# Heads two at a time on the two halves of the array, and a new order of loads, modulation and down products in a two-block transformer kernel

## The chip, the cores and the metric

The kernel runs on one core of one Trainium2 chip, in one launch. A time is the device time of a run in microseconds. The kernel before takes 1041.57 us, the median of three runs (1040.76 to 1041.62). The core's engines are TensorE (PE, with the loading of its weights listed apart as PEld), VectorE (DVE), ScalarE (ACT), GpSimd (POOL) and SyncE (SP), which issues nearly all of the transfers.

## The reference, cut to what matters

One sequence of 256 tokens, width 1024, passes through two transformer blocks. The first has two SwiGLU feed-forwards and, between them, a mixer of causal attention and a convolution; each of the three is modulated by numbers that are computed from a vector `c`. The second has a mixer with two attention branches and gates, a feed-forward with squared ReLU, and a gated projection at the end.

```
# block 1
mod = (silu(c) @ w_ada + b_ada).reshape(3, 3, 1024)
x = x + 0.5 * mod[0, 2] * swiglu(modulate(x, ...), w13[0], w2[0])    # 1024 -> 2 x 2816 -> 1024
x = x + mod[1, 2] * hybrid_mixer(modulate(x, ...), ...)              # 8 heads, values 64 wide
x = x + 0.5 * mod[2, 2] * swiglu(modulate(x, ...), w13[1], w2[1])
# block 2
z = rmsnorm(x, norm_mix_g) @ w_in            # qa ka va | qb kb vb | ga gb
y_a = mixer_a(qa, ka, va, ...) @ w_out_a     # 8 heads of 128
y_b = mixer_b(qb, kb, vb, rel_bias) @ w_out_b
# mixer_b: 4 heads of 64 in each of 3 dilated windows, softmax with a bias
#          by distance; the three are joined by their log-sum-exp
x = x + (sigmoid(ga + b) * y_a + sigmoid(gb + b) * y_b) @ w_out
x = x + square(relu(rmsnorm(x, norm_mlp_g) @ w_ff1)) @ w_ff2         # 1024 -> 4096 -> 1024
x = x + sigmoid(rmsnorm(x, norm_ple_g) @ w_ple_gate) * (p @ w_ple)
return rmsnorm(x, final_norm_g)
```

## The kernel before, in words

The activations lie transposed, 128 features on the partitions and 256 tokens in the row, in eight slices `d` of 128 features. Each fp32 weight that is used in a large product is split into two parts: ScalarE casts it to a high part `hi` (line 141), VectorE subtracts for a low part `lo` (line 142). A product is then three matmuls with 128x128 weights and 256 columns (`mm3`, lines 152 to 154). The small matmuls of the attention heads are plain fp32.

The stages on the time axis: start (to 31 us), first feed-forward (31 to 226), first mixer (226 to 399), second feed-forward (399 to 594), second mixer (594 to 827, with branch B in 704 to 764), the feed-forward of block 2, here the mlp (827 to 1002.6), and the end with the gate `pg` and the last norm.

The order of the instructions on each engine is set by the framework's scheduler from the order in which the code is written and from modelled times. Tiles come from pools with a fixed number of buffers; a transfer or a computation that needs a new buffer waits till an old one is free.

*Feed-forwards* (`stream_ffn`, lines 382 to 412). In each iteration `make` computes two slices of the hidden layer: products `gu` (or `u`), then `s` on ScalarE, `m` on VectorE, and the split of `m` into `mh` (ScalarE, line 174) and `ml` (VectorE, line 175). `second` multiplies the slices of the iteration before into the eight slices of the output, two to each of four banks `acc0` to `acc3`. Its weight, the down weight, is loaded right behind `make` (line 407). After the last `second`, `finish` adds each slice to the residual (line 416 or 421), from which the sum of squares for the next norm is built: `squares` (line 331) on ScalarE, the adding of six of them on POOL (line 333), and two that go to PE's `nrm_ps` directly (line 342). Where the next norm's factor comes later (`gained`), `hh` and `hl` (lines 377, 378) follow from the residual at once.

*Modulation.* `ada_rest` spreads parts of `silu(c) @ w_ada` over the iterations: 2 MB of weights from SyncE's queue, eight multiplications by VectorE (lines 267, 269), two casts to bf16 pieces `ada_b` on ScalarE (line 273) with two subtractions on VectorE (line 274), and, an iteration later, twelve matmuls `ada_ps` with one column (line 279). Its tuple says how many parts begin at each iteration.

*Heads.* `_stages` runs scores, transposition and values of successive heads as a pipeline, and `_interleave` mixes it with other products. In the first mixer the 64 values of a head fill half of the columns of the array (lines 777, 779); a bank `bo` takes two heads. In branch B, the 64 channels of a head are half of the rows in the scores `bs` (line 1106) and half of the columns in the values `bob` (line 1135); there are eight stages, each of one head and one half of the queries. Per stage come the bias from a table (`bias_tile`), the softmax (line 1111 and on), four transposes `bt` and one copy `pT`. Branch A's output product `ya` (`out_a`) and, after it, the gates `gab` run beside it.

Of the kernel before, what the change touches and what calls it, by code (L numbers as in the profile page):

```python
# [8 lines left out]
F32 = mybir.dt.float32  # L9
# [9 lines left out]
P = 128  # L19
# [42 lines left out]
def tile_two_blocks(ctx: ExitStack, tc: tile.TileContext, t: dict, out: bass.AP):  # L62
# [321 lines left out]
    def stream_ffn(nit, make, w2, finish, extra=None, at=None):  # L384
        with tc.tile_pool(name="mp", bufs=2) as mp:
# [3 lines left out]
            def second(i, mh, ml, w):  # L389
                for q in range(4):  # L390
                    for d in (2 * q, 2 * q + 1):
                        ps = acc[q][:, (d % 2) * T:(d % 2) * T + T]
                        for j in range(2):
                            mm3(ps, w[0][:, j, d * P:(d + 1) * P], w[1][:, j, d * P:(d + 1) * P], mh[:, j, :], ml[:, j, :],
                                i == 0 and j == 0 and d % 2 == 0, i == nit - 1 and j == 1)
                    if i == nit - 1:
# [3 lines left out]
            prev = None  # L400
            for i in range(nit):
# [10 lines left out]
            second(*prev)  # L412
# [178 lines left out]
    def mixer_one(px, tmp2):  # L591
# [36 lines left out]
        def latent():  # L628
# [114 lines left out]
            bo = {}  # L743
# [20 lines left out]
            def turn_p(hd, sm):  # L764
# [3 lines left out]
                pT = tmp2.tile([P, 384], F32, tag="pT", name="pT")  # L768
# [3 lines left out]
            def values(hd, pT):  # L772
                j = hd % 2
                if j == 0:
                    bo[0] = bankA("bo")
                o = bo[0][j * 64:j * 64 + 64, :]
                pe.matmul(o[:, 0:T], lhsT=vN[:, 0, hd * 64:hd * 64 + 64], rhs=pT[:, 0:T], start=True, stop=False,
                          skip_group_check=True)
                pe.matmul(o[:, P:T], lhsT=vN[:, 1, hd * 64:hd * 64 + 64], rhs=pT[:, T:384], start=False, stop=True,
                          skip_group_check=True)  # L780
                if j:
                    hilo(bo[0][:, :T], oaH[:, hd // 2, :], oaL[:, hd // 2, :])
# [103 lines left out]
    def bias_near(px, j):  # L886

        stg = px.tile([P, 80], F32, tag="bias_s", name="bias_s", bufs=2)
# [10 lines left out]
    def bias_tile(px, j, qt, stg):  # L899

        bt = px.tile([P, 512], F32, tag="bias", name="bias", bufs=2)
# [13 lines left out]
    swiglu(h, t["ffn_w13"][0][1], t["ffn_w2"][0][1], gt(2), ada_rest(ada_plan[12:], (1,)), fill=bias_rows, at=(16, 16))  # L915


    def mixer_two(px, tmp2):
# [20 lines left out]
        rtab = [px.tile([P, 2, 256], F32, tag="bias", name="rtab", bufs=2) for _ in range(2)]  # L939
# [155 lines left out]
        def scores_b(i):  # L1095
            j, qt = divmod(i, 2)
            pr_, jj = divmod(j, 2)
# [260 lines left out]
```

## Time and profile before

| | before |
|---|---|
| median of 3 runs | 1041.57 us |
| the profiled execution, whole | 1041.2 us |
| its span | 1039.4 us |
| PE busy | 1010.6 us, 97% |
| DVE, ACT, POOL busy | 71%, 54%, 3% |
| bytes moved | 215.41 MB, mean 207 GB/s |

The span reaches from the first to the last instruction of the profile; the execution has 1.8 us around it. Busy time of PE counts an instruction from its start to its modelled end, and matmuls overlap (one that is listed with 0.28 us has its successor start after 0.12), so waiting and pace are read from the starts. Text in square brackets behind a row of the timeline is the idle time before it and what ended it.

### The profile page before, as it was taken

Reading aid. Unit: us, or ns where it says so; the run is one execution under the profiler, and the core shown is the slowest. Engines: PE = TensorE matmul, PEld = TensorE weight load, DVE = VectorE, ACT = ScalarE, POOL = GpSimd, SP = SyncE. Lnnn points to the kernel's source line nnn. Section 1 sums busy time; section 2 is a strip of 40 time slices with the busy share of each in tenths; the row PEclk is TensorE's granted clock in tenths of the full one; section 3 lists DMA queues with packets and bytes.
Section 4 is the critical chain, followed back from the end, with each engine's and each line's share of the span. In section 5 each row is a group of like instructions: output and inputs, shape, how many; then the busy total and the mean of one; then the engine's idle time right before and its main releaser. Section 6 shows DMA issues by size and latency. Waiting matters only on the chain.

```text
span 1039.4 us, 20303 instructions
## 1 busy us (share of the span) xinstructions
PE 1010.6 (97%) x8332; PEld 976.3 (94%) x8332; DVE 741.4 (71%) x1414; ACT 557.1 (54%) x1036; POOL 35.0 (3%) x47
## 2 busy tenths in 40 slices
PE   6999999999999999999999999999999999999996
PEld 3799999999999998999999999999999999999996
DVE  4789998657977998965455689665467875655565
ACT  5564544447656456644444555544365674555453
POOL 0000000010000011000000100001100100000010
PEclk9999999999999999999999999999999999999998
DMA  9799899425655886986464444535325796566311
GB/s 358 276 386 333 303 347 370 142 78 182 200 187 161 274 283 220 343 301 203 163 215 143 137 141 133 163 122 158 119 83 188 240 317 203 187 203 203 123 61 41
DMA packets 161301, 215.41 MB, mean 207 GB/s; under 512 B 6206, under 2 KB 129877, under 8 KB 161080
## 3 DMA queue, kind: packets, MB, share of 16 engines
q1 hardware_dynamic: 159346, 212.58, 61.5%
q10 hardware_dynamic: 1862, 1.53, 0.5%
q8 instruction: 65, 1.06, 0.4%
q14 instruction: 28, 0.23, 0.1%
HBM read 210.63 MB, written 3.47 MB: 206 GB/s over the span
## 4 chain that ended last, share of the span: by engine, by line
PE 84%; DVE 9%; ACT 3%; DMA 2%; issue 1%; POOL 0%; ACTq 0%; DVEq 0%; POOLq 0%; SPq 0%
PE gu L152 8%; PE gu L153 8%; PE gu L154 8%; PE acc L152 6%; PE acc L153 6%; PE acc L154 6%; DVE lo L142 3%; PE u L154 2%; PE u L153 2%; PE u L152 2%; PE gab L152 2%; PE gab L154 1%; PE gab L153 1%; ACT hi L141 1%; PE gl L153 1%
## 5 line engine op out<-in xcount | busy, mean ns | idle before, releaser
L142 DVE TENSOR_TENSOR lo<-raw,hi 128x512 fp32r<-128x512 f32 (+2 forms) x454 | 395.5, 902 | 97.6 <-ACT hi L141 96.6
L141 ACT CAST hi<-raw 128x512 fp32r<-128x512 f32 (+2 forms) x454 | 336.9, 786 | 216.5 <-PE acc L153 76.9
L152 PE MATMUL gu<-hh,hi 128*128 128x256 f32 x704 | 198.1, 282 | 0.0
L153 PE MATMUL gu<-hl,hi 128*128 128x256 f32 x704 | 196.7, 280 | 0.1
L154 PE MATMUL gu<-hh,lo 128*128 128x256 f32 x704 | 196.7, 280 | 0.0
L152 PE MATMUL acc<-mh,hi 128*128 128x256 f32 x608 | 168.3, 278 | 2.3 <-ACT mh L174 2.3
L153 PE MATMUL acc<-ml,hi 128*128 128x256 f32 x608 | 168.6, 278 | 0.0
L154 PE MATMUL acc<-mh,lo 128*128 128x256 f32 x608 | 168.4, 277 | 0.0
L152 PEld LDWEIGHTS gu<-hh,hi 128*128 128x128 f32 x704 | 132.8, 189 | 0.7 <-issue 0.5
L153 PEld LDWEIGHTS gu<-hl,hi 128*128 128x128 f32 x704 | 132.8, 189 | 0.7 <-issue 0.5
L154 PEld LDWEIGHTS gu<-hh,lo 128*128 128x128 f32 x704 | 132.9, 189 | 0.2 <-DVE lo L142 0.2
L152 PEld LDWEIGHTS acc<-mh,hi 128*128 128x128 f32 x608 | 114.0, 188 | 2.7 <-ACT mh L174 2.7
L153 PEld LDWEIGHTS acc<-ml,hi 128*128 128x128 f32 x608 | 114.1, 188 | 0.2 <-DVE ml L175 0.2
L154 PEld LDWEIGHTS acc<-mh,lo 128*128 128x128 f32 x608 | 114.2, 188 | 0.0
L269 DVE SCALAR_TENSOR_TENSOR ada_acc<-ada,c_act,ada_acc 128x512 f32<-128x512 f32 x98 | 73.4, 749 | 2.6 <-DMA ada<-in_w_ada_dram 0.9
L152 PE MATMUL u<-hh,hi 128*128 128x256 f32 x256 | 71.0, 277 | 0.0
L153 PE MATMUL u<-hl,hi 128*128 128x256 f32 x256 | 70.9, 277 | 0.0
L154 PE MATMUL u<-hh,lo 128*128 128x256 f32 x256 | 70.8, 277 | 0.0
L88 ACT ACTIVATE s<-gu 128x256 f32<-128x256 f32 x44 | 16.7, 383 | 74.7 <-PE gu L154 74.6
L333 POOL TENSOR_TENSOR ssum<-ssum,sq 128x256 f32<-128x256 f32 x25 | 23.4, 936 | 806.5 <-ACT sq L331 805.6
L153 PEld LDWEIGHTS u<-hl,hi 128*128 128x128 f32 x256 | 48.1, 188 | 0.2 <-DVE hl L378 0.2
L152 PEld LDWEIGHTS u<-hh,hi 128*128 128x128 f32 x256 | 48.1, 188 | 0.0
(379 smaller groups left out, 2222.7 us busy)
## 6 DMA issues: line engine op xcount, KB each, us to landing
raw<-in_ffn_w_dram SPq DMA_DIRECT2D x64, 1024.0 KB
raw<-in_w_in_dram SPq DMA_DIRECT2D x37, 1024.0 KB
raw<-in_w_ff_dram SPq DMA_DIRECT2D x32, 1024.0 KB
ada<-in_w_ada_dram SPq DMA_DIRECT2D x28, 1024.0 KB
raw<-in_w_out_dram SPq DMA_DIRECT2D x8, 1024.0 KB
ada<-in_w_ada_dram SPq DMA_DIRECT2D x8, 768.0 KB
raw<-in_w_branch_dram SPq DMA_DIRECT2D x8, 512.0 KB
raw<-in_w_out_a_dram SPq DMA_DIRECT2D x4, 1024.0 KB
```

The costliest lines, as they stand in the source:

```text
L88: last_table[0] = act.activation(*args, **kw).ins
L141: act.copy(hi[:, sl], raw[:, sl])
L142: vec.tensor_tensor(out=lo[:, sl], in0=raw[:, sl], in1=hi[:, sl].bitcast(F32), op=ALU.subtract)
L152: pe.matmul(ps, lhsT=wh, rhs=xh, start=start, stop=False, skip_group_check=True)
L153: pe.matmul(ps, lhsT=wh, rhs=xl, start=False, stop=False, skip_group_check=True)
L154: pe.matmul(ps, lhsT=wl, rhs=xh, start=False, stop=stop, skip_group_check=True)
L269: vec.scalar_tensor_tensor(out=acc, in0=wv[:, k, :], scalar=c_act[:, k0 + k:k0 + k + 1], in1=acc, op0=ALU.mult, op1=ALU.add)
L333: pool.tensor_tensor(out=s[0], in0=s[0], in1=sq, op=ALU.add)
```

## The change

Five edits:

1. Branch B works on two heads in one stage, four stages in place of eight. The matmuls of the two heads alternate: in the scores between the two halves of the rows (two banks), in the values between the two halves of the columns. The bias gets 3 buffers and its small tile 4; `sm` and `pT` of the second head take room of other tiles; `bob` lies in the other set of banks.
2. The values of the first mixer are computed for two heads at once, alternating between the halves of the columns, with three buffers for `pT`.
3. In a feed-forward the down weight of an iteration is loaded behind the next iteration's strips.
4. The last two down products are one: a bank gets the products of both iterations before the next bank begins.
5. The two parts of the modulation in the second feed-forward begin at iterations 3 and 4, not 0 and 1.

The number of matmuls is the same.

```diff
@@ stream_ffn
-            def second(i, mh, ml, w):
+            def second(*its):
                 for q in range(4):
                     for d in (2 * q, 2 * q + 1):
                         ps = acc[q][:, (d % 2) * T:(d % 2) * T + T]
-                        for j in range(2):
-                            mm3(ps, w[0][:, j, d * P:(d + 1) * P], ...)
-                    if i == nit - 1:
+                        for i, mh, ml, w in its:
+                            for j in range(2):
+                                mm3(ps, w[0][:, j, d * P:(d + 1) * P], ...)
+                    if its[-1][0] == nit - 1:
                         for d in (2 * q, 2 * q + 1):
                             finish(d, acc[q][:, (d % 2) * T:(d % 2) * T + T])
...
+            down = lambda i: cols(w2, 0, D, 2 * i, 2, at=at, wp=mp, bufs=2)
+            mids = []
             for i in range(nit):
...
                 make(i, mh, ml, mp)
-                if prev is not None:
-                    second(*prev)
-                prev = (i, mh, ml, cols(w2, 0, D, 2 * i, 2, at=at, wp=mp, bufs=2))
+                if i:
+                    mids[-1] += (down(i - 1),)
+                if 0 < i < nit - 1:
+                    second(mids.pop())
+                mids.append((i, mh, ml))
...
-            second(*prev)
+            mids[-1] += (down(nit - 1),)
+
+            second(*mids)
@@ mixer_one, values
+                pTs[hd % 2] = pT
+                if hd % 2 == 0:
+                    return
+                bo = bankA("bo")
+                for k, (a, e) in enumerate(((0, T), (T, 384))):
+                    for j in range(2):
+                        c = (hd - 1 + j) * 64
+                        pe.matmul(bo[j * 64:j * 64 + 64, k * P:T], lhsT=vN[:, k, c:c + 64], rhs=pTs[j][:, a:e],
+                                  start=k == 0, stop=k == 1, skip_group_check=True)
@@ second feed-forward
-    swiglu(h, ..., ada_rest(ada_plan[12:], (1,)), fill=bias_rows, at=(16, 16))
+    swiglu(h, ..., ada_rest(ada_plan[12:], (0, 0, 0, 1, 1)), fill=bias_rows, at=(16, 16))
@@ scores_b
+                a, e, ks = ((0, 256, slice(0, T)), (256, 384, qs), (384, 512, qs))[g]
+                for jj in range(2):
+                    rows = slice(jj * 64, jj * 64 + 64)
+                    pe.matmul(bs[jj][:, a:e], lhsT=qB[rows, 2 * g + pr_, qs], rhs=kB[rows, 2 * g + pr_, ks], ...)
@@ values_b_of
             for c in range(4):
-                v = vB[(0, 0, 1, 2)[c]][:, (0, 1, qt, qt)[c], j * 64:(j + 1) * 64]
-                pe.matmul(bo[jj * 64:jj * 64 + 64, qt * P:(qt + 1) * P], lhsT=v, rhs=pT[:, c * P:(c + 1) * P],
-                          start=c == 0, stop=c == 3, skip_group_check=True)
+                for jj in range(2):
+                    j = 2 * pr_ + jj
+                    v = vB[(0, 0, 1, 2)[c]][:, (0, 1, qt, qt)[c], j * 64:(j + 1) * 64]
+                    pe.matmul(bo[jj * 64:jj * 64 + 64, qt * P:(qt + 1) * P], lhsT=v, rhs=pTs[jj][:, c * P:(c + 1) * P],
+                              start=c == 0, stop=c == 3, skip_group_check=True)
@@ the stages of branch B
-        _interleave(_stages(8, (scores_b, turn_b, values_b_of), {}), out_a())
+        _interleave(_stages(4, (scores_b, turn_b, values_b_of), {}), out_a())
```

In the order of PE, in branch B, one stage's scores (`bs`) and the values (`bob`) of an earlier stage, between products of `ya` and `gab`, stand so before:

```order
L154 MATMUL ya_8786<-oAH_7152,lo_8777 128x256
L1106 MATMUL bs_8847<-qkB_7148 128x256
L1106 MATMUL bs_8847<-qkB_7148 128x128 x2
L1135 MATMUL bob_8648<-pT_8816,vB0_7149 64x128 x2
L1135 MATMUL bob_8648<-pT_8816,vB1_7150 64x128
L1135 MATMUL bob_8648<-pT_8816,vB2_7151 64x128
L152 MATMUL gab_9049<-hh_7106,hi_9027 128x256
```

and so after (all six score matmuls, and the first five of eight for values):

```order
L154 MATMUL ya_8876<-oAH_7152,lo_8867 128x256
L1114 MATMUL bs_8949<-qkB_7148 128x256
L1114 MATMUL bs_8950<-qkB_7148 128x256
L1114 MATMUL bs_8949<-qkB_7148 128x128
L1114 MATMUL bs_8950<-qkB_7148 128x128
L1114 MATMUL bs_8949<-qkB_7148 128x128
L1114 MATMUL bs_8950<-qkB_7148 128x128
L1151 MATMUL bob_8976<-pT_8906,vB0_7149 64x128
L1151 MATMUL bob_8976<-pT_8913,vB0_7149 64x128
L1151 MATMUL bob_8976<-pT_8906,vB0_7149 64x128
L1151 MATMUL bob_8976<-pT_8913,vB0_7149 64x128
L1151 MATMUL bob_8976<-pT_8906,vB1_7150 64x128
```

Where one head's three score matmuls and four value matmuls stood in a row, those of two heads now alternate, and there are half as many such places.

At the end of the first feed-forward PE's rows stand so before, from bank `acc2` to bank `acc3`:

```order
L152 MATMUL acc2_439<-mh_2415,hi_2593 128x256
L153 MATMUL acc2_439<-ml_2416,hi_2593 128x256
L154 MATMUL acc2_439<-mh_2415,lo_2594 128x256
L152 MATMUL acc3_440<-mh_2415,hi_2593 128x256
L153 MATMUL acc3_440<-ml_2416,hi_2593 128x256
L154 MATMUL acc3_440<-mh_2415,lo_2594 128x256
```

and so after, in bank `acc3`:

```order
L152 MATMUL acc3_440<-mh_2190,hi_2537 128x256
L153 MATMUL acc3_440<-ml_2191,hi_2537 128x256
L154 MATMUL acc3_440<-mh_2190,lo_2538 128x256
L152 MATMUL acc3_440<-mh_2407,hi_2560 128x256
L153 MATMUL acc3_440<-ml_2408,hi_2560 128x256
L154 MATMUL acc3_440<-mh_2407,lo_2561 128x256
```

`mh_2415` and `mh_2407` are the last iteration's slices, `mh_2190` the ones before; the bank now takes both before it is done, where the earlier one had been multiplied into all four banks first.

On ScalarE, at the start of the second feed-forward, stand behind the table load before:

```order
L88 ACTIVATE s<-gu 128x256 x2
L273 CAST ada_b<-ada_acc 128x512
L174 CAST mh<-m 128x256 x2
L141 CAST hi<-raw 128x1024
L273 CAST ada_b<-ada_acc 128x512
L141 CAST hi<-raw 128x1024 x5
L88 ACTIVATE s<-gu 128x256
L174 CAST mh<-m 128x256
```

and after:

```order
L88 ACTIVATE s<-gu 128x256 x2
L174 CAST mh<-m 128x256 x2
L141 CAST hi<-raw 128x1024 x6
L88 ACTIVATE s<-gu 128x256
L174 CAST mh<-m 128x256
L141 CAST hi<-raw 128x1024 x3
```

Both casts to `ada_b` are gone from between `s` and `mh` and behind it; they now come with the iterations 3 and 4.

## Rows read from the trace of the kernel before

**Rows 1.** The page, part 1: busy time and instructions of each engine.

```profile
PE 1010.6 (97%) x8332; PEld 976.3 (94%) x8332; DVE 741.4 (71%) x1414; ACT 557.1 (54%) x1036; POOL 35.0 (3%) x47
```

**Rows 2.** Windows by stage: us, busy time (x instructions) of each engine, PEclk, DMA.

```profile
31.00:226.00 195.00, 193.76 (x1694) 190.99 (x1692) 162.63 (x264) 102.12 (x151) 3.46 (x5) 1.00 0.82 286
...
704.00:764.00 60.00, 59.87 (x457) 54.65 (x456) 32.99 (x75) 28.14 (x55) 7.79 (x12) 1.00 0.43 136
```

**Rows 3.** List of waits, engine PE: us in total, times, longest.

```profile
PE acc L152 <- ACT mh L174: 2.3, 2, 1.3
...
PE nrm_ps L342 <- POOL ssum L333: 1.7, 2, 1.5
...
PE ada_ps L279 <- ACT ada_b L273: 1.6, 2, 1.0
...
PE pg L153 <- DVE hl L378: 0.7, 2, 0.4
PE qa L171 <- DVE hl L378: 0.6, 1, 0.6
```

**Rows 4.** Timeline of PE, branch B: start us, us, line, operation, out<-in, count.

```profile
712.35 0.28 PE L154 MATMUL ya<-oAH,lo 128*128 128x256 f32 x1
...
713.84 0.28 PE L153 MATMUL ya<-oAL,hi 128*128 128x256 f32 x1
...
716.43 0.28 PE L154 MATMUL ya<-oAH,lo 128*128 128x256 f32 x1
...
717.89 0.28 PE L153 MATMUL ya<-oAL,hi 128*128 128x256 f32 x1
...
735.15 0.28 PE L154 MATMUL ya<-oAH,lo 128*128 128x256 f32 x1
735.36 1.14 PE L1106 MATMUL bs<-qkB 64*128 64x256 f32 x6
736.43 1.09 PE L1135 MATMUL bob<-pT,vB 128*64 128x128 f32 x8
...
737.67 0.28 PE L153 MATMUL gab<-hl,hi 128*128 128x256 f32 x1
```

**Rows 5.** Timeline of PE, values of one head in the first mixer.

```profile
313.23 0.28 PE L152 MATMUL gl<-hh,hi 128*128 128x256 f32 x1
313.46 0.65 PE L777 MATMUL bo<-pT,vN 128*64 128x256 f32 x2
...
314.48 0.28 PE L154 MATMUL gl<-hh,lo 128*128 128x256 f32 x1
```

**Rows 6.** Timeline of PE, second feed-forward.

```profile
499.11 0.28 PE L152 MATMUL gu<-hh,hi 128*128 128x256 f32 x1
...
501.58 0.28 PE L152 MATMUL acc<-mh,hi 128*128 128x256 f32 x1
```

**Rows 7.** Windows of the second feed-forward and of the mlp.

```profile
502.00:593.00 91.00, 91.00 (x805) 91.00 (x804) 49.49 (x67) 43.80 (x68) 0.70 (x1) 1.00 0.54 174
845.00:1000.00 155.00, 155.00 (x1370) 155.00 (x1369) 90.47 (x146) 76.95 (x144) 0.00 (x0) 1.00 0.55 181
```

**Rows 8.** Tile `ada_ps`, 399 to 594 us: duration ns, first and last start.

```profile
L279 PE MATMUL ada_ps<-one,ada_b x32: 163/163/178, 398.9 to 456.2; 128*128 128x1 bf16 x32
```

**Rows 9.** Timeline of POOL and PE, end of the first feed-forward.

```profile
223.05 3.16 POOL L333 TENSOR_TENSOR ssum<-ssum,sq 128x256 f32<-128x256 f32 x4 [0.35 <-ACT sq L331]
...
226.26 0.70 PE L342 MATMUL nrm_ps<-ssum,ones 128*128 128x256 f32 x2 [1.51 <-POOL ssum L333]
```

**Rows 10.** Line 378, all its instructions: duration ns min/median/max.

```profile
L378 DVE SCALAR_TENSOR_TENSOR hl<-xT,colB,hh x24: 470/482/1012, 591.2 to 1006.0; 128x256 fp32r<-128x256 f32 x24
```

**Rows 11.** Timeline of PE and ScalarE, start of the second feed-forward.

```profile
419.60 0.28 PE L154 MATMUL gu<-hh,lo 128*128 128x256 f32 x1
...
420.19 0.61 ACT L273 CAST ada_b<-ada_acc 128x512 bf16<-128x512 f32 x1
...
421.16 0.72 PE L152 MATMUL acc<-mh,hi 128*128 128x256 f32 x4 [1.28 <-ACT mh L174]
```

More of the change, by code (lines that the diff above doesn't have):

```diff
@@ L886, in bias_near @@
     def bias_near(px, j):
[L888 removed]
+        stg = px.tile([P, 80], F32, tag="bias_s", name="bias_s", bufs=4)
         for rr in range(2):
@@ L938, in mixer_two @@
         act.dma_start(out=gg[:, 1, :], in_=row_bc(t["k_norm_g_2"], P))
-        rtab = [px.tile([P, 2, 256], F32, tag="bias", name="rtab", bufs=2) for _ in range(2)]
+        rtab = [px.tile([P, 2, 256], F32, tag="bias", name="rtab", bufs=3) for _ in range(2)]
         blk = lambda z: z.rearrange("p a (f s n) -> p a f s n", f=2, s=2)
@@ L1095, in scores_b @@
         def scores_b(i):
[L1096 to L1098 removed]
+            pr_, qt = divmod(i, 2)
+            qs = slice(qt * P, (qt + 1) * P)
             if qt == 0:
[L1100 to L1103 removed]
+                stage_b.update({jj: bias_near(px, 2 * pr_ + jj) for jj in range(2)})
@@ L1104, in scores_b @@
+            bias = [bias_tile(px, 2 * pr_ + jj, qt, stage_b[jj]) for jj in range(2)]
+            bs = [bankA("bs") for _ in range(2)]
             for g in range(3):
-                dst, ks = ((bs[:, 0:256], slice(0, T)), (bs[:, 256:384], qs), (bs[:, 384:512], qs))[g]
-                pe.matmul(dst, lhsT=qB[lo_:hi_, 2 * g + pr_, qs], rhs=kB[lo_:hi_, 2 * g + pr_, ks], start=True, stop=True)
-            sm = tmp2.tile([P, 512], F32, tag="sm", name="sm", bufs=3)
-            mx = tmp.tile([P, 1], F32, tag="mx1", name="mx1")
@@ L1119, in turn_b @@
-        def turn_b(i, sm):
-            bt = bankA("bt")
-            for c in range(4):
-                tr(bt[:, c * P:(c + 1) * P], sm[:, c * P:(c + 1) * P])
-            pT = tmp2.tile([P, 512], F32, tag="pT", name="pT")
-            act.copy(pT, bt)
-            return i, pT
-        def values_b_of(i, pT):
-            j, qt = divmod(i, 2)
-            pr_, jj = divmod(j, 2)
-            if i % 4 == 0:
-                bo_b[0] = bankA("bob")
+                a, e, ks = ((0, 256, slice(0, T)), (256, 384, qs), (384, 512, qs))[g]
@@ new lines, in scores_b, with turn_b, values_b_of @@
+            return i, sms
+        def turn_b(i, sms):
+            pTs = []
+            for jj, sm in enumerate(sms):
+                bt = bankA("bt")
+                for c in range(4):
+                    tr(bt[:, c * P:(c + 1) * P], sm[:, c * P:(c + 1) * P])
+                pT = tmp2.tile([P, 512], F32, tag="pT" if jj == 0 else "sq2", name="pT")
+                act.copy(pT, bt)
+                pTs.append(pT)
+            return i, pTs
+        def values_b_of(i, pTs):
+            pr_, qt = divmod(i, 2)
+            if qt == 0:
+                bo_b[0] = bankB("bob")
```

54 lines of the change are left out of this document (22 added, 32 removed).

## The prediction

> **What bounds the kernel now.** I read the page first: TensorE (PE) is busy 1010.6 of 1039.4 us, VectorE 71%, ScalarE 54% [rows 1]. So time is won only where PE waits, where an instruction takes PE more than its columns need, or where the pace of the products changes. The windows by stage say the same of the place that the change touches most: between 704 and 764 us, branch B, PE is busy 59.87 of 60 us [rows 2]. Next came the list of PE's waits [rows 3]. The entries that this change can touch are short: 2.3 us for `mh`, 1.7 for the sum of squares, 1.6 for the bf16 pieces of the modulation, 0.7 and 0.6 for `hl`. None is for a weight of a feed-forward. Last the timeline, product by product: around the small matmuls of the heads, which use half of the array [rows 4, 5], and for the pace of the large ones [rows 6, 7].
>
> The pace has two levels. A 128x256 product starts every 0.1176 us up to 501.58 us (21 steps from 499.11 to 501.58 [rows 6]) and every 0.113 us from there to 593, and again through the mlp (91 us hold 805 products, 155 us hold 1370 [rows 7]). No wait stands at the switch, and I don't know what makes it. It matters below.
>
> **Heads by pairs in branch B.** An fp32 matmul is recorded as two passes: a score block has 6, a value block 8. From the product ahead of a lone score block to the second one behind it are 713.84 - 712.35 = 1.49 us. Two steps of the pace are 0.24, so the block costs 1.25 us; a lone value block costs 717.89 - 716.43 - 0.24 = 1.22. Where the two stand side by side, 735.15 to 737.67, they cost 2.28 and not 2.47 [rows 4]. One change of shape saved is thus worth 0.19 us, and a lone block has two. That leaves 0.87 and 0.84 us for the passes themselves: 0.105 for 128 columns, 0.22 for 256.
>
> The change takes no matmul away; it halves the number of blocks. By the order of instructions there are 30 changes between the whole and half of the array in branch B before, and 19 after (the first score pair is cut by four transposes, the last value pair by three products of `gab`). 11 x 0.19 = 2.1 us. This part is nearly certain.
>
> What else it gives hangs on something that no row shows: two halves of the array used one right behind the other. If the first pass in one half runs beside the second pass in the other, a value pair needs 9 slots in place of 16, 0.73 us less, and a score pair some 1.15 us in place of 1.74, 0.6 less. Four of each make 5.3 us, 4.8 with the cut pairs. If nothing overlaps it is 0; if a change of half costs as much as a change of shape it is a loss (rival 2). I take 70%, 3.4 us: the passes of a block follow each other at the time that their columns need, so what holds the next one is the array, and half of that is free. Branch B: -5.5 us, between -2.1 and -8.9 (all passes halved).
>
> The Trainium skill (TensorEngine Tiling (Array Packing), Key Properties) says that a change of tiling mode drains TensorE, a mere change of tile not, and that different tiles load weights and multiply in parallel. The 0.19 us fits the first half; no row here shows the second. By it branch B would give the whole 6.9 us.
>
> What pairs cost: both softmaxes of a stage start together, so the second head's transposes are ready one chain of VectorE and ScalarE later. Beside it PE has 24 to 48 products of `ya` or `gab`, 2.8 to 5.6 us. At the first pair there is least in hand; I put +0.5 us, 0 to +1.5.
>
> **Heads by pairs in the mixer's values.** A block there costs 314.48 - 313.23 - 0.24 = 1.01 us [rows 5], 0.63 of it passes. An unbroken pair saves 0.43 by overlap. In the new order one pair is unbroken; in the other three the first matmul stands alone, products or transposes follow, and then three in a row, 0.22 less each. That makes 1.1 us, of which again 70%, 0.75; and of 16 changes of shape 14 stay, 0.4. Together -1.1 us, -0.3 to -1.6.
>
> **Joined last down products.** So far the last two down products are two rounds over four banks, 12 products (1.4 us) to a bank and round. Now a bank gets its 24 in one go, 2.8 us, and its two residuals, with what the next norm needs of them, come at that distance. POOL adds squares at 0.79 us each (3.16 for 4), falls behind, and PE waits 1.51 us for it at 226.26 [rows 9]; with 2.8 us for two adds, 1.6, it keeps up. In the same way `hl` takes 0.47 to 1.01 us [rows 10], and PE waits 0.6 us for it in `qa` and 0.7 in `pg` [rows 3]. The waits are 3.0 us in all; six slow restarts of some 0.1 us (an estimate: half of a change of shape) make 3.6. The last bank's residuals come as late as ever, but `qa` and `pg` have 18 products, 2.1 us, that don't need them. I take -3.0 us, 0 to -4. Late next is `hl` of the last two slices. The last `m`, `mh` and `ml` lose cover too: 22 products, 2.6 us, stand ahead of their first use, where it was 48. From the last product of `gu` at 419.60 to `mh` in use at 421.16 are 1.6 us, 0.61 of it the cast of something else [rows 11], so this costs nothing, at most 0.5.
>
> **Later modulation.** At 421.16 PE waits 1.28 us for `mh`, and on ScalarE the cast to `ada_b`, 0.61 us, runs from 420.19 on, ahead of it [rows 11]. In the new order the casts and the 16 multiplications on VectorE leave that place; two more `lo` pieces come in. -0.7 us, 0 to -1.5. At their new place, two iterations later, 96 products of `gu` cover them.
>
> The 1.6 us of waits for `ada_b` [rows 3] are those of the modulation's parts beside the first mixer's gates. There 13 products of `gl` or `po` now stand between the pieces. -0.8 us, 0 to -1.6.
>
> **Loads in order of use.** In SyncE's queue a down weight now stands behind the next iteration's strips. PE waits for no such weight today [rows 3], so there is nothing to win; 96 products of cover, 11 us, go, and VectorE, which splits the weights, is busy 162.63 of 195 us in the first feed-forward [rows 2]. Value 0, -0.2 to +2.
>
> **Pace.** The quick level began 45 us after the last interruption of the second feed-forward by the modulation's matmuls, at 456.2 [rows 8]. That one moves two iterations of 17 us later. If the distance counts, 300 products lose 0.0045 us each, 1.35 us; if the place counts, nothing. +0.7; the far end is rival 3.
>
> **Sum.** -5.5 + 0.5 - 1.1 - 3.0 - 0.7 - 0.8 + 0 + 0.7 = -9.9 us on the profiled execution's own 1041.2 us (span 1039.4 and 1.8 around it): 1031.3. The median of the three runs is 0.4 higher: 1031.7.
>
> **Rivals.**
> 1. *The halves run one after another.* Only changes of shape are saved. For: a pass streams its columns at the full rate of its input, and the matmuls keep their order in every row. Against: half of the array idles in each. 3.4 + 0.75 less gained: 1035.8.
> 2. *Each change of half is a break like a change of shape.* For: wherever the used part of the array changes, the rows show 0.19 us. Against: those are changes between unlike shapes. By the new order there are 19 such changes in the scores, 27 in branch B's values and 9 in the mixer's; 55 x 0.19 = 10.4 us on top of rival 1: 1046.2, slower. It decides from 0.1 us a change, where the other gains of 5.8 us are eaten.
> 3. *The quick pace doesn't come.* 805 and 1370 products ran at it [rows 7]; 2175 x 0.0045 = 9.8 us, of which 0.7 is counted: 1040.8, no change. For: it came without visible cause. Against: three runs of the kernel lie within 0.9 us, so it is no matter of chance from run to run, and the mlp's order is the same up to its last iterations.
> 4. *The joined products give nothing*, since the last bank alone sets the wait: 1034.7.
>
> **How the numbers follow.** Forecast 0.55, rival 1 0.18, rivals 2 and 3 0.10 each, rival 4 0.07. A measurement of this kernel can tell 0.2%, 2.1 us, from no change. Faster by more than that: nearly all of the forecast and of rivals 1 and 4, and little of rival 3, 0.79. Within it: most of rival 3, 0.08. Slower: rival 2, and down weights late in the first feed-forward with the slow pace, 0.13. The range goes from the larger gains together (-6.9 - 1.6 - 4 - 1.5 - 1.6, about -16: 1025.5) to rival 3 (1040.8); I set it to 1025 and 1040.5.
>
> **What would show it.** In the new trace: value pairs of 16 passes in about 1.0 us (overlap), 1.7 (rival 1) or over 2.5 (rival 2); no wait of `nrm_ps` for `ssum` at the first feed-forward's end, and none for `hl` in `qa` and `pg`; a wait for `mh` near 421 us of 0.7 or less; the mlp's products still every 0.113 us, and not 0.1176. The prediction is wrong if branch B isn't shorter by 2 us or more, if PE waits for `lo` in the first feed-forward, or if the pace has changed.

## The result and the profile after

The changed kernel takes 1027.09 us, the median of four runs (1025.27 to 1028.21), against 1041.16 for the kernel before beside it: a ratio of 0.9867 (95% interval 0.9846 to 0.9887). Measured again with six runs it took 1026.08, ratio 0.9862 (0.9839 to 0.9886). The prediction was 1031.7 us, within 1025 to 1040.5: the direction and the range held, the gain of 14 us was 4 larger than the 9.9 of the sum.

The page's first part, after, against [rows 1]:

```profile
PE 1000.1 (97%) x8332; PEld 967.7 (94%) x8332; DVE 742.8 (72%) x1414; ACT 555.8 (54%) x1036; POOL 34.6 (3%) x47
```

The span is 13.4 us shorter, and PE is busy 10.5 us less with the same number of instructions: so I read most of the gain not as waiting that is gone but as matmuls that overlap each other.

Where it went is read from the first and last start of some tiles' products. The view of the tiles, one row of each; behind the count stand min/median/max of the duration in ns, then the first and the last start:

```profile
L152 PE MATMUL pw<-pH,hi x16: 279/280/469, 225.1 to 231.5; 128*128 128x256 f32 x16
...
L152 PE MATMUL po<-mg,hi x64: 276/279/365, 372.4 to 395.3; 128*128 128x256 f32 x64
...
L169 PE MATMUL qa<-hi,hh x80: 280/281/373, 590.8 to 628.2; 128*128 128x256 f32 x80
...
L169 PE MATMUL va<-hi,hh x16: 281/281/468, 598.0 to 603.5; 128*128 128x256 f32 x16
...
L1114 PE MATMUL bs<-qkB x48: 269/272/480, 699.9 to 733.7; 64*128 64x128 f32 x32, 64*128 64x256 f32 x16
...
L152 PE MATMUL gab<-hh,hi x128: 278/279/384, 734.9 to 788.2; 128*128 128x256 f32 x128
```

The same view of the kernel before, its two rows for branch B:

```profile
L1106 PE MATMUL bs<-qkB x48: 269/272/480, 704.2 to 756.7; 64*128 64x128 f32 x32, 64*128 64x256 f32 x16
...
L152 PE MATMUL gab<-hh,hi x128: 276/279/388, 737.4 to 801.3; 128*128 128x256 f32 x128
```

With these rows, and those of `u` and `pg`, the stages compare so:

| from | to | before, us | after, us | difference |
|---|---|---|---|---|
| start of the span | first `pw` (end of the first feed-forward) | 226.6 | 225.1 | -1.5 |
| first `pw` | last `po` (first mixer) | 171.8 | 170.2 | -1.6 |
| last `po` | first `qa` (second feed-forward) | 195.7 | 195.5 | -0.2 |
| first `qa` | first `va` (end of the second feed-forward) | 8.3 | 7.2 | -1.1 |
| first `va` | first `bs` of branch B | 101.8 | 101.9 | +0.1 |
| first `bs` of branch B | last `gab` | 97.1 | 88.3 | -8.8 |
| last `gab` | first `u` | 24.0 | 24.1 | +0.1 |
| first `u` | first `pg` (mlp) | 177.3 | 177.0 | -0.3 |
| first `pg` | end of the span | 36.8 | 36.7 | -0.1 |

Two thirds lie in branch B: 801.3 - 704.2 = 97.1 us before, 788.2 - 699.9 = 88.3 after. The timeline of PE there, after, in the columns of [rows 4]:

```profile
709.14 0.28 PE L154 MATMUL ya<-oAH,lo 128*128 128x256 f32 x1
709.35 1.15 PE L1114 MATMUL bs<-qkB 64*128 64x256 f32 x12
...
710.65 0.28 PE L153 MATMUL ya<-oAL,hi 128*128 128x256 f32 x1
...
713.24 0.28 PE L154 MATMUL ya<-oAH,lo 128*128 128x256 f32 x1
713.45 1.09 PE L1151 MATMUL bob<-pT,vB 128*64 128x128 f32 x16
...
714.70 0.28 PE L153 MATMUL ya<-oAL,hi 128*128 128x256 f32 x1
```

Twelve passes of two heads' scores take 710.65 - 709.14 = 1.51 us with their neighbours, where one head's six took 1.49 [rows 4]; sixteen passes of values take 1.46, as one head's eight did. The second head costs next to nothing. In the single records of these blocks each pass of the second head starts 0.006 to 0.007 us behind the first head's, and in the value block so do the loads of the weights.

At the end of the first feed-forward, the timeline of POOL and PE, answering [rows 9]:

```profile
223.15 1.55 POOL L333 TENSOR_TENSOR ssum<-ssum,sq 128x256 f32<-128x256 f32 x2 [0.54 <-ACT sq L331]
...
224.76 0.70 PE L342 MATMUL nrm_ps<-ssum,ones 128*128 128x256 f32 x2
```

POOL adds in twos, with gaps, and is done by the time that PE asks; `nrm_ps` waits for nothing, where it waited 1.51 us. In PE's list of waits of the changed kernel there is no entry for `ssum`, and none for `hl` in `qa` or `pg`. What is left of [rows 3], and three entries that are new:

```profile
PE acc L152 <- ACT mh L174: 1.3, 3, 0.8
PE bt L178 <- DVE sm L767: 1.1, 1, 1.1
...
PE bt L178 <- DVE se L1125: 0.5, 1, 0.5
PE bt L178 <- DVE sm L1126: 0.3, 1, 0.3
```

The three for `bt`, the transposes, are the price of pairs: PE waits for a softmax 0.3 us at the first stage of branch B, 0.5 at the last, and 1.1 at the last pair of the first mixer (line 767), where the kernel before and val_single, with single heads there, have no such wait. The wait for `mh` at the start of the second feed-forward, answering [rows 11], is 0.77 us and not 1.28:

```profile
418.65 0.74 PE L152 MATMUL acc<-mh,hi 128*128 128x256 f32 x4 [0.77 <-ACT mh L174]
```

### The profile page after: what moved, and what is told of

It reads as the page before. It is cut to its first block, busy times and chain, and to the rows that moved or that the text cites. A ratio compares the mean times of both kernels' runs of the same rounds, so it can differ in the third digit from the quotient of the medians.

```text
span 1026.0 us, 20282 instructions
## 1 busy us (share of the span) xinstructions
PE 1000.1 (97%) x8332; PEld 967.7 (94%) x8332; DVE 742.8 (72%) x1414; ACT 555.8 (54%) x1036; POOL 34.6 (3%) x47
## 3 DMA queue, kind: packets, MB, share of 16 engines
q8 instruction: 65, 1.06, 0.4%
## 4 chain that ended last, share of the span: by engine, by line
PE 89%; DVE 5%; ACT 3%; DMA 1%; issue 1%; SPq 0%; POOL 0%; DVEq 0%; ACTq 0%; POOLq 0%
PE gu L152 8%; PE gu L153 8%; PE gu L154 8%; PE acc L152 7%; PE acc L153 6%; PE acc L154 6%; PE u L153 2%; PE u L152 2%; PE u L154 2%; PE po L152 2%; PE po L153 1%; PE po L154 1%; PE gab L154 1%; PE gab L153 1%; PE gab L152 1%; PE gl L153 1%
## 5 line engine op out<-in xcount | busy, mean ns | idle before, releaser
L333 POOL TENSOR_TENSOR ssum<-ssum,sq 128x256 f32<-128x256 f32 x25 | 23.5, 938 | 811.5 <-ACT sq L331 810.7
```

The lines of the kernel that those rows point to most:

```text
L333: pool.tensor_tensor(out=s[0], in0=s[0], in1=sq, op=ALU.add)
```

## The experiments

Ratios are to the kernel before, run on the same chip in the same rounds; the changed kernel's own ratio is 0.9862 to 0.9867 there, and 0.001 is 1 us. The runs of one kernel scatter by 2 to 9 us, the intervals are 0.0015 to 0.003 to either side, and a difference below 2 us is read from the traces or left open. In what follows a product counts as quick where the next 128x256 product starts within 0.1155 us, halfway between the two levels of the pace; between the levels lie 0.0048 us a product.

### Is the gain of branch B the overlap of the two halves?

**b_pairs**: the kernel before with the stages of two heads in branch B and nothing else.

```diff
-        _interleave(_stages(8, (scores_b, turn_b, values_b_of), {}), out_a())
+        _interleave(_stages(4, (scores_b, turn_b, values_b_of), {}), out_a())
```

> The kernel before with one part of the change alone: branch B by pairs of heads, four stages. Theory: the two halves of the array run fully side by side, so that a pair's block takes the time of one head's block; branch B then loses 8.7 us (as read between the two traces) and the kernel comes out 8.7 us (8 to 9.5) under the kernel before, about 1032.4. Rival: part of what branch B seems to win is the pace of the products or other edits that arrive there; then this kernel gains 5 us or less, 1036 or more.

Measured: 1031.97 us, ratio 0.9922 (0.9904 to 0.9941), 8.1 us under the kernel before. The view of the tiles gives first and last starts:

```profile
L1107 PE MATMUL bs<-qkB x48: 269/272/480, 703.6 to 737.5; 64*128 64x128 f32 x32, 64*128 64x256 f32 x16
...
L152 PE MATMUL gab<-hh,hi x128: 278/279/384, 738.7 to 792.0; 128*128 128x256 f32 x128
```

From the first `bs` to the last `gab` are 88.4 us, as in the changed kernel (88.3). So the 8.8 us belong to this edit alone; the rival falls.

**b_by_head**: the changed kernel, with one head's matmuls behind the other's.

```diff
-            for c in range(4):
-                for jj in range(2):
+            for jj in range(2):
+                for c in range(4):
```

(and the same in the scores)

> The changed kernel with branch B still in stages of two heads, but the matmuls of the two heads one head after the other and not alternating. Theory: what wins is that each pass in one half stands right beside a pass in the other; one head after the other leaves only the seam between them to overlap, so 4 x (0.87 + 0.84) = 6.8 us less about 0.1 at each seam come back: 6 us over the changed kernel, about 1033, a value block of 16 passes 1.9 us long. Rival: PE runs ahead into the other half over several matmuls, or what counts is only that there are fewer changes of shape; then the time stays within 1 us of the changed kernel's 1027.1.

Measured: 1028.57 us, ratio 0.9893 (0.9877 to 0.9908): some 3 us over the changed kernel by the ratios, neither the theory's 6 nor the rival's 0 to 1. In its trace the first `bs` (699.1) and the last `gab` (790.3) lie 91.2 us apart, 2.9 more than in the changed kernel. The timeline of PE shows a value block of 16 passes:

```profile
713.38 0.28 PE L154 MATMUL ya<-oAH,lo 128*128 128x256 f32 x1
713.59 1.58 PE L1151 MATMUL bob<-pT,vB 128*64 128x128 f32 x16
...
715.32 0.28 PE L153 MATMUL ya<-oAL,hi 128*128 128x256 f32 x1
```

From the product ahead to the second behind are 1.94 us, where alternating matmuls need 1.46 and two blocks in a row would need some 2.3 (1.46 and eight more passes of 0.105). In the single records one pass starts every 0.11 us up to 714.08; from there to 714.46 two series run beside each other, and then one again. PE thus takes up the second head's work while three passes of the first are still to come, but no earlier. My theory, that only neighbours at the seam overlap, was wrong. The Trainium skill (TensorE: Matmul & The Clock Gate, Part 3: Packing small matmuls) says that matmuls start and end strictly in the program's order. These records differ from it: for eight passes of each head to come out, the second head's first matmul must have begun at 714.08 and the first head's fourth at 714.29.

**b_two_two**: values in groups of two matmuls of a head.

```diff
-            for c in range(4):
-                for jj in range(2):
+            for c2 in (0, 2):
+                for jj in range(2):
+                    for c in (c2, c2 + 1):
```

> One look: the changed kernel with branch B's values in groups of two matmuls of one head, then two of the other (scores alternate as in the change). With one matmul in turn, 16 passes took 1.02 us to the next product; with four in turn 1.51, and there the second head's first pass began three passes before the first head's last. Theory: PE takes up work for the other half while at most about three passes of the first are still to come; with groups of two matmuls (four passes) only the first pass stands alone, so a block takes 1.1 us. Rival: matmuls start strictly in turn and only neighbours overlap; then each of three seams overlaps one pass, 13 slots, 1.4 us.

Measured: 1030.12 us in a single run, which gives no ratio; the timeline of PE at a value block:

```profile
715.62 0.28 PE L154 MATMUL ya<-oAH,lo 128*128 128x256 f32 x1
715.83 1.14 PE L1152 MATMUL bob<-pT,vB 128*64 128x128 f32 x16
...
717.13 0.28 PE L153 MATMUL ya<-oAL,hi 128*128 128x256 f32 x1
```

1.51 us with the neighbours, 0.05 over strict alternation; the block itself (715.83 to the next product) takes 1.07 us, near the theory's 1.1, and not 1.4. Groups of up to two fp32 matmuls overlap almost wholly, groups of four by two fifths (0.36 of 0.84 us).

### What do cut pairs cost?

In the changed kernel three of the mixer's four value pairs are cut. The timeline of PE at one of them:

```profile
305.38 0.65 PE L787 MATMUL bo<-pT,vN 128*64 128x256 f32 x2
...
306.19 0.28 PE L154 MATMUL gl<-hh,lo 128*128 128x256 f32 x1
306.30 0.28 PE L152 MATMUL gl<-hh,hi 128*128 128x256 f32 x1
306.51 0.86 PE L787 MATMUL bo<-pT,vN 128*64 128x256 f32 x6
...
307.53 0.28 PE L154 MATMUL gl<-hh,lo 128*128 128x256 f32 x1
```

The first head's first matmul, two passes, stands alone from 305.38 on, three products of `gl` follow, and then the other six passes.

**second_first**: the head that is ready last is multiplied first, so that the pair can't begin before both are there.

```diff
-                    for j in range(2):
+                    for j in (1, 0):
                         c = (hd - 1 + j) * 64
...
-                for jj in range(2):
+                for jj in (1, 0):
                     j = 2 * pr_ + jj
```

> The changed kernel with the two heads of each value pair in the other order, in the first mixer and in branch B: the head whose probabilities come last is multiplied first, so that no pair is cut open by other products. Theory: a cut pair costs a block more (0.38 us for its changes of shape) and loses the overlap of its first passes (0.2 to 0.4 us); four of them, and the half overlap of the first pair, make 2.5 us: about 1024.6. Rival: the wait for the second head then stands on PE in place of the cut, since the other products are not brought ahead; no difference, 1027.

Measured: 1024.27 us, ratio 0.9854 (0.9834 to 0.9875). The timeline of PE, the same pair and then the last one:

```profile
305.17 0.28 PE L153 MATMUL gl<-hl,hi 128*128 128x256 f32 x1
305.37 0.87 PE L787 MATMUL bo<-pT,vN 128*64 128x256 f32 x8
...
306.40 0.28 PE L152 MATMUL gl<-hh,hi 128*128 128x256 f32 x1
...
321.48 0.70 PE L178 MATMUL bt<-ident,sm 128*128 128x128 f32 x3 [1.18 <-DVE sm L767]
323.23 0.87 PE L787 MATMUL bo<-pT,vN 128*64 128x256 f32 x8 [1.05 <-ACT pT L775]
...
324.26 0.28 PE L153 MATMUL y<-ocL,hi 128*128 128x256 f32 x1
```

The pair now takes 306.40 - 305.17 = 1.23 us with its neighbours, as a single head did before (1.25 [rows 5]). Set product by product against the changed kernel's trace, counted from the first `pw`, this one is 0.2 us ahead at the mixer's first pair and 0.8 at each of the next two, and gives 0.5 back at the last. There PE waits 1.05 us for the second head's probabilities, on top of the wait for the softmax (1.18 us here) that the changed kernel has too: theory and rival each had a part.

**second_again**: the same kernel once more, beside the next one.

> The kernel of the run second_first once more, beside the last one. Theory: unbroken pairs are worth 2 to 3 us over the changed kernel, so the ratio is 0.984 to 0.9855 and branch B's and the mixer's stretches are as short as in its first trace. Rival: the first run was helped by the share of quick products; then the ratio comes back to 0.9865.

Measured: 1024.20 us, ratio 0.9853 (0.9838 to 0.9869). By the ratios it lies 1 to 1.5 us under the changed kernel both times. The intervals overlap, so it is the better kernel by its medians, and the size of the step is not settled. Of the stretches, branch B is as short as in the first trace (87.8 us both times, 88.3 in the changed kernel). The first mixer is not: 171.5 us (first `pw` 224.3, last `po` 395.8), where it was 168.2. Windows of 6.7 us there, first of second_again, then of second_first (the third figure from the end is PEclk):

```profile
322.70:329.40 6.70, 6.32 (x30) 5.61 (x31) 4.48 (x7) 3.07 (x5) 0.00 (x0) 0.50 0.57 172
```

```profile
322.70:329.40 6.70, 6.17 (x54) 5.85 (x55) 6.59 (x11) 3.54 (x7) 0.00 (x0) 1.00 0.57 168
```

In second_again the granted clock was 0.50 (1.2 GHz) from 322.6 to 329.4 us: 30 records of PE's matmuls in place of 54, and a product every 0.213 us. Just before, PE had waited 1.18 us for the softmax, and the clock fell within the second wait, of 1.06 us. The same two waits stand in second_first, and there the clock stayed at 1.00. Nearly 3 of the 3.3 us lie in this stretch. Whether the longer waiting at the last pair brings such a fall about is not shown by one profile out of two.

**best2**: as second_first, but the last pair of the mixer in the old order.

```diff
-                    for j in (1, 0):
+                    for j in ((0, 1) if hd == 7 else (1, 0)):
```

> The kernel of the run second_first with one difference: the last pair of the first mixer keeps the first head ahead, since there PE has no other products and waited 1.1 us for the second head's probabilities before the pair began. Theory: the first head's matmul then fills part of that wait, 0.5 us less than second_first (ratio 0.985). Rival: the wait only moves behind the first matmul, no difference from second_first.

Measured: 1025.37 us, ratio 0.9865 (0.9845 to 0.9886): not better than second_first. The timeline of PE at the last pair:

```profile
323.52 0.33 PE L178 MATMUL bt<-ident,sm 128*128 128x128 f32 x1 [1.13 <-DVE sm L767]
323.78 0.65 PE L787 MATMUL bo<-pT,vN 128*64 128x256 f32 x2
...
325.79 0.86 PE L787 MATMUL bo<-pT,vN 128*64 128x256 f32 x6
...
326.80 0.28 PE L153 MATMUL y<-ocL,hi 128*128 128x256 f32 x1
```

The wait for the probabilities is gone: nine products of `y` stand between the first head's first matmul and the other six passes. The two traces must be set beside each other by the work done, since this one's start is 1.4 us longer (the granted clock was 0.50 from 30.3 to 33.7 us). From the last pair's first transpose on, the pair and ten products of `y` take 326.80 - 323.52 = 3.28 us here; in second_first the pair and one product take 324.26 - 321.48 = 2.78, and nine more at 0.118 make it 3.84. So at this place 0.5 us are won, as the theory said. They show neither at the mixer's end (168.4 us, 168.2 in second_first, which has 80 more quick products there, worth 0.4) nor in the time; the rival has the time on its side, though not by its reason.

**val_single**: the changed kernel with the mixer's values by single heads again.

```diff
-                bo = bankA("bo")
-                for k, (a, e) in enumerate(((0, T), (T, 384))):
-                    for j in range(2):
...
+                o = bo[0][j * 64:j * 64 + 64, :]
```

> The changed kernel with the first mixer's values again one head at a time, as in the kernel before. Theory: only one of the four pairs stood unbroken and that one half overlapped, so the pairs there were worth 0.8 us (0.3 to 1.2): 0.8 over the changed kernel. Rival: the whole 1.6 us that the first mixer is shorter by came from the pairs, and the filling of the waits for ada_b gave nothing: 1.6 over it, with the waits for ada_b still absent.

Measured: 1028.59 us, ratio 0.9889 (0.9861 to 0.9918), 2.5 us over the changed kernel by the medians. In its trace the first mixer is 171.6 us long (first `pw` 225.2, last `po` 396.8), 1.4 more than the changed kernel's 170.2. That is hardly more than the same code's own scatter: with the changed kernel's mixer it was 170.2 to 170.8 us long in after_again, no_join, mod_early and old_loads, and 171.2 to 171.5 in b_by_head, b_two_two and ada_two. And the waits for the modulation's pieces are back:

```profile
PE ada_ps L279 <- ACT ada_b L273: 1.4, 2, 0.8
...
PE ada_ps L279 <- DVE ada_b L274: 0.5, 1, 0.5
```

So these two terms hang together: with the new place of the values in PE's order 13 products fall between those pieces. But they don't always cover the wait: it is 0 in the changed kernel's first profile, 0.4 in after_again, and 0.8 to 1.0 us in the three longer mixers just named. In return the wait of 1.1 us for `sm` at the last pair is gone here. From the kernel before to the changed one the mixer's -1.6 us are thus 2.2 of waits for `ada_b` saved, 1.1 for `sm` added, and some 0.5 that are left for the overlap and the changes of shape. The ratios, with intervals of 0.003, don't narrow it.

### The joined products, the loads and the modulation

**no_join**: the last two down products one after the other.

```diff
-            second(*mids)
+            for it in mids:
+                second(it)
```

> The changed kernel with the last two down products one after the other again in all three feed-forwards, all else as changed (loads in order of use too). Theory: the joined products are worth the 1.5, 1.1 and some 0.5 us that the three ends differ by between the traces, about 3 us: 1030. PE then waits again for the sum of squares at the first feed-forward's end (over 1 us) and for hl in qa and pg. Rival: the last bank sets the wait alone, or the ends differ for another reason: 1027 to 1027.7, and no such waits.

Measured: 1030.10 us, ratio 0.9902 (0.9884 to 0.9919), 3.5 to 4 us over the changed kernel. PE's list of waits:

```profile
PE nrm_ps L342 <- POOL ssum L333: 1.8, 2, 1.6
...
PE pg L153 <- DVE hl L378: 0.7, 2, 0.4
PE qa L171 <- DVE hl L378: 0.6, 1, 0.6
```

They are the entries of [rows 3], within 0.1 us. The theory holds; the joined order is worth its three waits, and how much beyond them is open. The first feed-forward as a whole is no longer than the changed kernel's (193.5 and 193.6 us), though PE waits 1.6 us at its end: 560 of its products ran at the quick pace in this profile, against 197, which is worth 1.7 us.

**old_loads**: each down weight loaded at its old place, the products still joined.

```diff
-                if i:
-                    mids[-1] += (down(i - 1),)
...
-                mids.append((i, mh, ml))
+                mids.append((i, mh, ml, down(i)))
```

> The changed kernel with each down weight loaded and split at its old place, right behind its own iteration's products, and everything else as changed (the last two down products joined). Theory: PE never waited for a down weight and doesn't now, so the order of the loads is worth nothing: within 1 us of the changed kernel (ratio 0.986 to 0.987). Rival: the new order keeps the strips of the next iteration ahead of a down weight that isn't needed yet; with the old order PE waits for lo of a strip in the first feed-forward, 1 to 3 us over the changed kernel.

Measured: 1027.08 us, ratio 0.9879 (0.9863 to 0.9895). The two readings disagree by a microsecond (equal to the changed kernel's first median, 0.0012 to 0.0017 above its ratios), and PE's waits show no entry for a `lo`, neither here nor in the changed kernel. Worth nothing or about one microsecond; no wait shows where it would lie. In its trace the first feed-forward is even 1.1 us shorter (192.5), but with 559 quick products against 197, worth 1.7 us: at the same pace it would be 0.6 longer.

**mod_early**: the second feed-forward's modulation at iterations 0 and 1.

```diff
-... ada_rest(ada_plan[12:], (0, 0, 0, 1, 1)), fill=bias_rows, at=(16, 16))
+... ada_rest(ada_plan[12:], (1,)), fill=bias_rows, at=(16, 16))
```

> The changed kernel with the second feed-forward's two parts of the modulation at iterations 0 and 1 again. Theory: the cast of ada_b stands ahead of mh again, PE waits 1.3 us instead of 0.8 near 418 us, and the second feed-forward is 0.7 us longer: 0.7 over the changed kernel. Rival: the earlier interruptions let the quick pace come back earlier, and the time is the same or less.

Measured: 1026.70 us, ratio 0.9862 (0.9837 to 0.9887), the changed kernel's own. Its list of waits has

```profile
PE acc L152 <- ACT mh L174: 1.8, 3, 1.3
```

and so the 0.5 us of the longer wait are there, as the theory said, but they don't show in the time. The stage is 195.7 us long in this trace, 1.3 more than in b_by_head (194.4), which is the changed kernel there and whose granted clock was at 0.50 for as long; 824 quick products against 1093 make up the whole of the 1.3.

### What sets the pace of the products?

**after_again**: the changed kernel once more.

> The changed kernel itself, measured again beside the kernel before as a base for the others. The ratio was 0.9867 (0.9846 to 0.9887); it should lie in that interval again. The runs of a kernel scatter by up to 5 us; theory: most of it is the share of the products that run at the quick pace (0.113 us) and not the slow one (0.118), which changes from one execution to the next; then this profile has its switches at other places than the first one. Rival: the switches are fixed by the order of the instructions and stand where they stood (58, 74, 420, 484, 530 and 828 us).

Measured: 1026.08 us, as above. In the second feed-forward and the mlp its quick stretches are those of the first profile. That first profile, in windows (length, then PE busy and its count of records):

```profile
421.00:484.00 63.00, 63.00 (x559) 63.00 (x558) 48.65 (x60) 33.77 (x47) 0.00 (x0) 1.00 0.83 285
531.00:590.00 59.00, 58.74 (x517) 58.54 (x517) 34.68 (x51) 29.43 (x50) 2.28 (x3) 1.00 0.52 161
828.00:989.00 161.00, 160.93 (x1418) 160.57 (x1417) 96.82 (x158) 82.64 (x155) 2.28 (x3) 1.00 0.55 178
```

0.113 to 0.114 us a product in all three; after_again has 558, 518 and 1416 in the same windows. The rival held for this pair of profiles. It does not hold in general. The two profiles of the kernel second_first, windows of the mlp, first

```profile
828.00:843.00 15.00, 15.00 (x130) 15.00 (x129) 9.36 (x15) 7.60 (x14) 0.00 (x0) 1.00 0.92 304
```

and then, in the run second_again,

```profile
828.00:843.00 15.00, 15.00 (x135) 15.00 (x134) 11.25 (x19) 9.78 (x17) 0.00 (x0) 1.00 0.97 313
```

130 records against 135 in 15 us of the same stretch of the mlp (its first `u` stood at 808.0 and 810.7): the first ran slow, the second quick. The level is no property of the order alone.

The pace is not all that differs between profiles of one kernel. The granted clock falls to 0.50 (1.2 GHz) in each of them behind the first mixer, where PE is doing the 24 matmuls `bias_ps` or has just done them, but not for the same time: from 407.8 to 411.3 us in the kernel before, from 401.6 to 408.4 in the changed one, from 405.3 to 408.7 in b_by_head. The last two have the same code there and nearly the same number of quick products (1080 and 1093), and their second feed-forwards take 195.5 and 194.4 us. In five of the fourteen profiles the clock falls at some 30 us too, about the end of a wait of 2.0 to 2.7 us for `ada_acc`; in these the start takes 32.3 to 33.7 us to the first `gu`, in the others 30.8 to 31.6. And over all recorded runs of kernels that ran more than three times, the 11 with a mean granted clock of 0.992 or less lie on average 2.0 us above their kernel's mean, the 41 with 0.995 or more 0.8 us below it. So part of the scatter that I put down to the pace is the clock's.

**ada_two**: the modulation's matmuls of two parts in one place, so that they break into the products half as often.

```diff
+            if len(begun) > 1 or not todo:
+                for g in begun:
+                    next(g, None)
+                begun = []
```

> The changed kernel with the modulation's small matmuls (ada_ps) of two parts done together: 4 interruptions in the first feed-forward and not 8, 1 in the second and not 2. Multiplications, casts and loads stay where they were. Theory: such an interruption drops the products to the slow pace (0.118 us), and the quick one (0.113) comes back only at the start of a later round of down products; with half as many, some 600 products more run quick, 2.5 us less (0.5 to 5) than the changed kernel, and the first feed-forward of the trace has quick stretches of 17 us and more. Rival: the level has nothing to do with interruptions; no difference (within 0.5 us).

Measured: 1027.01 us, ratio 0.9871 (0.9847 to 0.9895), no gain. In the first feed-forward, windows of this kernel and then of the changed one:

```profile
74.00:215.00 141.00, 141.00 (x1272) 140.83 (x1270) 122.76 (x189) 71.80 (x104) 0.00 (x0) 1.00 0.83 289
```

```profile
74.00:215.00 141.00, 141.00 (x1268) 140.65 (x1267) 123.91 (x189) 70.44 (x102) 0.00 (x0) 1.00 0.84 288
```

Both run slow throughout, with 1272 and 1268 records in 141 us, so halving the interruptions brought no quick stretch. On the other side no_join, old_loads and mod_early have quick stretches in this feed-forward with all eight of them. My theory, that the interruptions keep the pace slow, falls. What sets the level stays open.

## Why the prediction was right, and where its sizes were off

**Branch B** was the term that was mis-sized: -5.5 + 0.5 put, -8.8 measured in the stage and -8.1 by b_pairs. The 11 changes of shape that I counted are gone in the trace, too. The step that failed is the one of the slots: I let the first pass in one half run beside the second pass in the other and took 70% of that. In fact passes and weight loads of both halves go in lockstep, so the passes of the second head, 4 x (0.87 + 0.84) = 6.8 us, vanish whole; with 2.1 that is 8.9, the far end of the range that I gave for this term. As the stage also holds 0.8 us of new waits, what was won in it is 9.6, of which some 0.3 is the pace; the last 0.4 are not accounted for. The sentence of the Trainium skill (TensorEngine Tiling (Array Packing), Key Properties) that I had set beside it, that tiles load and multiply in parallel, was nearer than my 70%; the 6.9 us that I worked out by it were too small because of my slots and not of the rule. Rivals 1 and 2 are ruled out by the blocks of 1.51 and 1.46 us.

**The price of pairs** was put at +0.5, at the first stage; it is 0.8 us of waits of `bt`, 0.3 there and 0.5 at the last. For the mixer's pairs I put nothing, and there it is 1.1 us.

**Mixer's values and the filled waits**: -1.1 and -0.8 put, -1.6 measured in the stage. They are not two terms: taking the pairs back brings the waits back. The near agreement is luck in part: the waits saved were 2.2 us and not 1.6 (the 0.6 for `ada_b` from VectorE I had left out), and the wait of 1.1 us that the pairs brought stood in no sum.

**Joined down products**: -3.0 put. The three ends are 1.5, 1.1 and, with the pace of the mlp in it, some 0.4 us shorter; no_join gives 3.5 to 4 for the whole. Right in the mechanism, point by point, and in size within what the runs can tell.

**Later modulation**: -0.7 put. The wait fell from 1.28 to 0.77 us, -0.5, a little short of the 0.7 or less that I had named as a sign; by mod_early it makes no difference that can be measured. That the whole stage is only 0.2 us shorter, with 0.7 more from the pace, fits the granted clock: it was at 0.50 for longer there than before, which b_by_head prices at some 1.0 us. The prediction had no term for it.

**Loads**: 0 put; the runs leave 0 to about 1.

**Pace**: +0.7 put, and it came out the other way: 559 and 517 products of the second feed-forward ran quick, 805 and a short stretch before (by the single records 1080 against 931), which is 0.7 us gained. By my own list a changed pace was a sign of being wrong; it was met, if by little. The argument behind the term failed twice. The distance of 45 us from an interruption was no rule: here the quick level came 28 us behind the last one, at 530 after 502. And "three runs lie within 0.9 us, so it is no matter of chance": eleven later runs of the kernel before lie between 1036.32 and 1045.44. So rival 3 was weighed with a reason against it that was no reason. That its 9.8 us didn't come is not explained by anything that I had argued. Pace and granted clock each make a part of the scatter; that they make all of it is not shown.

The stages sum to -13.4 us of span, 3.5 more than the forecast's 9.9. Branch B alone, 3.8 beyond its terms, makes this up; the other errors nearly cancel.

## What to carry to other kernels

If two matmuls use different halves of the array, put them next to each other, in turn: here the second then cost next to nothing, fp32 passes and weight loads included. In groups of four, one head after the other, they overlapped only over the last three passes. Let the operand that is ready last be used first, so that a scheduler can't cut the pair open; where PE has no other work at that place it waits instead, 1.05 us at the mixer's last pair. Set traces beside each other by the work done and not by the time since the start, and read the granted clock before a difference of a few microseconds is put down to an edit. Where a reduction over slices follows the last product, finish the slices at the distance that the reduction needs rather than in two quick rounds.

## What the runs showed of the hardware that was not expected

Sixteen passes of two heads take 1.02 us from the first to the next product, as eight of one head did. In groups of four matmuls the second head's passes begin three passes before the first head's end; in groups of two the whole block takes 1.07. A change between the whole and half of the array costs 0.19 us at each crossing, a change of half none that shows. The 128x256 products have two paces, 0.113 and 0.118 us, with a granted clock of 1.00 (2.4 GHz) in the windows of both; the pace can differ between two runs of the same instructions (135 and 130 records in 15 us). At a granted clock of 0.50 (1.2 GHz) such a product takes 0.213 us, and the fall can come in one run of a kernel and not in another (second_again, second_first).
